# Prompt scores from three float32r products instead of one float32 product

## The chip, the cores and the metric

One Trainium2 chip, of which the kernel uses one core. The metric is the time of one execution on the device in microseconds (us); three timed executions of the kernel before took 1303.28, 1303.49 and 1303.51 us, median 1303.49 us.

## What is computed

The kernel does one inference step of a decoder trunk of two layers, for a prompt group (1 sequence of 256 tokens) and a sample group (8 sequences of 1 token) that share the weights. Each layer is a half feed-forward block, a mixer (a short convolution in layer 0, a gated linear recurrence in layer 1), a cross-attention on a memory, and a second half feed-forward block. The change lies in the cross-attention, which for the prompt is, per layer:

```python
def mem_kv(mem, g_mem, w_kv):
    k, v = jnp.split(rmsnorm(mem, g_mem) @ w_kv, 2, axis=-1)
    return k.reshape(B, N, X_HEADS, X_HEAD_DIM), v.reshape(B, N, X_HEADS, X_HEAD_DIM)

def cross_attn(x, mk, mv, w_q, w_o):
    q = (x @ w_q).reshape(B, T, X_HEADS, X_HEAD_DIM)
    s = jnp.einsum('bthd,bnhd->bhtn', q, mk.astype(q.dtype)).astype(jnp.float32) / math.sqrt(X_HEAD_DIM)
    p = jax.nn.softmax(s, axis=-1).astype(x.dtype)
    o = jnp.einsum('bhtn,bnhd->bthd', p, mv.astype(x.dtype)).reshape(B, T, D)
    return o @ w_o
```

Here D is 1024, T is 256, N (memory rows) is 256, and there are 4 heads of 256. The prompt's keys and values come from `mem_kv`, the samples' from a cache in HBM. Everything is float32.

## The kernel before, in words

The activations are kept transposed: `xT` has the 1024 model columns on 8 tiles of 128 partitions, and 264 columns, 256 of the prompt and 8 of the samples, so that every projection serves both groups. Nearly all products on TensorE use the type float32r, which is cheap there but keeps fewer bits. To keep the precision, an operand is split into a float32r part `h` and the float32r remainder `l` (`x - h`), and a product is made of three passes, h·h, h·l and l·h. `mm3` (L305 to L310) issues the three passes; in the projections they are L308, L309 and L310. The weights of a projection come from HBM as `raw`; ScalarE casts them to `wh` (L107), and VectorE or GpSimd subtracts to get `wl` (L119). The class `Weights` keeps this ahead of the products, five weight tiles deep.

In attention, `project` first makes the queries of the four heads, `qTs[h]` (L833, a VectorE multiplication out of PSUM, 256 head columns on two 128-partition tiles by 264 tokens, float32). Then, head by head, `do_kv` makes keys and values (L847 to L849, 512 columns a pass, 48 passes a head) and ScalarE copies them out to `Kn` and `Vn` (L857). During these four heads the weights' remainders `wl` are made by GpSimd (`W.lo = ("p",)`), otherwise by VectorE. At the end of `do_kv` the values are split into `Vh` (L864, ScalarE) and `Vl` (L865, VectorE).

The rest of a head runs beside the products of the next head. `Flow` holds three lanes of Python generators. After every few matmuls the program calls `flow.tick()`, which first advances the weights and then lets every lane take one step, up to its next `yield`. Lane 1 holds for each head: `transpose_k` (TensorE turns `Kn` into the PSUM tile `pkt`, L877, and VectorE copies it to `KTt`, L881); `prompt_scores` (the scores `psc`, L929, then the softmax: row maximum L913 and L914 on VectorE, exponentials L288 on ScalarE, L919 and L921 on VectorE into `Pp`; then TensorE turns `Pp` into `ppt`, L943, which is split into `PTh`, L949, and `PTl`, L950); and `prompt_values` (the output `po`, twelve passes of `mm3`, then its parts `oh`, L965, and `ol`, L966). From the transposing step of a head to its scores there are two more ticks in between. Lane 0 holds the samples' attention: for each head, 16 products of cached keys with the query on VectorE (`junk`, L901), and when all four heads are done `sample_rest`: the maximum over rows `mxs` (L973), turned by TensorE (`pst`, L976), the maximum `top` (L977), spread out to `tops` (L978), a product with `tops` (L980), and so on to the samples' values `spv` (L1003). The cached keys and values come through a ring of four buffers.

The steps of the program give each instruction its rank, but each engine's final order is made when the program is built, by rank and by what is estimated to be ready, and it is then fixed: on the chip, an engine takes its instructions strictly in that order. A tile with a tag and `bufs=1` has one place in memory; the next tile with that tag waits until all readers of the one before are done. In the score step `psc` is written by four float32 matmuls (two token halves, two head halves), each with a 128x128 part of `qT` as its weights and 256 columns of `KTt` moving.

Last comes the output projection (`out_proj`), in which VectorE makes `wl` again. The fourth head's turn, scores and values fall into it.

Of the kernel before, what the change touches and what calls it, by code (L numbers as in the profile page):

```python
# [8 lines left out]
F32 = mybir.dt.float32  # L9
F32R = mybir.dt.float32r  # L10
# [6 lines left out]
P = 128  # L17
D = 1024
KT = D // P
T = 256  # L20
# [4 lines left out]
NMEM = 256  # L25
# [196 lines left out]
def trunk_step(ctx: ExitStack, tc: tile.TileContext, ins, consts, outs, stop=None):  # L222
    nc = tc.nc
# [10 lines left out]
    def aux_bank(name):  # L234
        return paux.tile([P, 512], F32, tag="aux", name=name)
# [70 lines left out]
    def mm3(ps, w, rh, rl, first, last, s=slice(None)):  # L306
        wh, wl = w
        nc.tensor.matmul(ps, wh[:, s], rh, start=first, stop=False)  # L308
        nc.tensor.matmul(ps, wh[:, s], rl, start=False, stop=False)  # L309
        nc.tensor.matmul(ps, wl[:, s], rh, start=False, stop=last)  # L310
# [496 lines left out]
    def attention(l, norm, nxt):  # L807
        with tc.tile_pool(name="at", bufs=1) as ap:
            mh = ap.tile([P, KT, NMEM], F32R, name="mh")
            ml = ap.tile([P, KT, NMEM], F32R, name="ml")  # L810
            KTt, Vn, qTs, PTp = {}, {}, {}, {}
            oh = ap.tile([P, KT, NC], F32R, name="oh")
            ol = ap.tile([P, KT, NC], F32R, name="ol")
            sc = ap.tile([P, XH, NI], F32, name="sc")
# [24 lines left out]
            def do_kv(h):  # L839
# [25 lines left out]
                nc.vector.tensor_sub(vl, vn, vh.bitcast(F32))  # L865
                Vn[h] = vh, vl
                flow.spawn(1, transpose_k(h, kn))
                flow.spawn(1, prompt_scores(h))
                flow.spawn(1, prompt_values(h))
                flow.tick()  # L870

            def transpose_k(h, kn):
                yield
                pt = aux_bank("pkt")
                for dt in range(2):
                    for nt in range(2):
                        nc.tensor.transpose(  # L877
                            pt[:, dt * NMEM + nt * P : dt * NMEM + nt * P + P], kn[:, nt, dt * P : dt * P + P], ident
                        )
                KTt[h] = ap.tile([P, 2, NMEM], F32, tag="KTt", name=f"KTt{h}", bufs=1)  # L880
                nc.vector.tensor_copy(KTt[h], pt.rearrange("p (t n) -> p t n", t=2))  # L881
                yield
                yield

# [24 lines left out]
            def softmax(src, npart, rows, name):  # L909
                pr = ap.tile([npart, rows, NMEM], F32, tag=f"P{name}", name=f"P{name}", bufs=1)  # L910
                mx = ap.tile([npart, rows], F32, tag=f"mx{name}", name=f"mx{name}", bufs=2)
                zs = ap.tile([npart, rows], F32, tag=f"zs{name}", name=f"zs{name}", bufs=2)
                nc.vector.reduce_max(mx, src, axis=AX.X)  # L913
                nc.vector.tensor_scalar(mx, mx, -1.0 / 16.0, None, op0=ALU.mult)  # L914
                for r in range(rows):
                    act(
                        pr[:, r], src[:, r], AF.Exp, bias=mx[:, r : r + 1], scale=1.0 / 16.0, accum_out=zs[:, r : r + 1]
                    )
                nc.vector.reciprocal(zs, zs)  # L919
                for r in range(rows):  # L920
                    nc.vector.tensor_scalar(pr[:, r], pr[:, r], zs[:, r : r + 1], None, op0=ALU.mult)  # L921
                return pr

            def prompt_scores(h):
                qT = qTs[h]
                ps = aux_bank("psc")
                for tt in range(2):
                    for dt in range(2):
                        nc.tensor.matmul(  # L929
                            ps[:, tt * NMEM : tt * NMEM + NMEM],  # L930
                            qT[:, dt, tt * P : tt * P + P],
                            KTt[h][:, dt],
                            start=dt == 0,
                            stop=dt == 1,
                        )
                pr = softmax(ps.rearrange("p (t n) -> p t n", t=2), P, 2, "p")
                yield
                yield
                yield
                pt = aux_bank("ppt")  # L940
                for nt in range(2):
                    for tt in range(2):
                        nc.tensor.transpose(  # L943
                            pt[:, nt * T + tt * P : nt * T + tt * P + P], pr[:, tt, nt * P : nt * P + P], ident
                        )
                ptv = pt.rearrange("p (t n) -> p t n", t=2)
                th = ap.tile([P, 2, T], F32R, tag="PTh", name="PTh", bufs=1)
                tl = ap.tile([P, 2, T], F32R, tag="PTl", name="PTl", bufs=1)
                nc.scalar.copy(th, ptv)  # L949
                nc.vector.tensor_sub(tl, ptv, th.bitcast(F32))  # L950
                PTp[h] = th, tl
                yield
# [484 lines left out]
    for l in range(2):  # L1437
        plan.append(("norm_ffn1", l, SILU, ffn, lambda l=l: reg_ffn("ffn1", l)))
        plan.append(("norm_mix", l, None if l == 0 else SIGMOID, rec if l else conv, reg_rec if l else reg_conv))
        plan.append(("norm_xattn", l, None, lambda n, x, l=l: attention(l, n, x), lambda l=l: reg_att(l)))  # L1440
        plan.append(("norm_ffn2", l, SILU, ffn, lambda l=l: reg_ffn("ffn2", l)))
# [71 lines left out]
```

## Time and profile before

| what | value |
|---|---|
| median of three executions | 1303.49 us |
| the profiled execution, by its own time | 1303.28 us |
| span of the profiled execution, first to last instruction | 1301.3 us |
| TensorE matmul (PE) busy | 1279.6 us, 98% |
| VectorE (DVE) busy | 824.1 us, 63% |
| ScalarE (ACT) busy | 694.5 us, 53% |
| GpSimd (POOL) busy | 293.5 us, 23% |
| cross-attention, layer 0, queries to the fourth head's output | about 314 to 411 us |
| cross-attention, layer 1 | about 981 to 1078 us |
| granted TensorE clock, mean | 0.997 of full speed |

PE, DVE, ACT and POOL stand for TensorE, VectorE, ScalarE and GpSimd; L929 is line 929 of the kernel; `psc<-KTt,qT` names the tile written and the tiles read. Times count from the first instruction. The profile counts one float32 matmul as two instructions. [...]

### The profile page before, as it was taken

Reading aid. Unit: us, or ns where it says so; the run is one execution under the profiler, and the core shown is the slowest. Engines: PE = TensorE matmul, PEld = TensorE weight load, DVE = VectorE, ACT = ScalarE, POOL = GpSimd, SP = SyncE. Lnnn points to the kernel's source line nnn. Section 1 sums busy time; section 2 is a strip of 40 time slices with the busy share of each in tenths; the row PEclk is TensorE's granted clock in tenths of the full one; section 3 lists DMA queues with packets and bytes.
Section 4 is the critical chain, followed back from the end, with each engine's and each line's share of the span. In section 5 each row is a group of like instructions: output and inputs, shape, how many; then the busy total and the mean of one; then the engine's idle time right before and its main releaser. Section 6 shows DMA issues by size and latency. Waiting matters only on the chain.

```text
span 1301.3 us, 25953 instructions
## 1 busy us (share of the span) xinstructions
PE 1279.6 (98%) x10310; PEld 1236.4 (95%) x10310; DVE 824.1 (63%) x1570; ACT 694.5 (53%) x1146; POOL 293.5 (23%) x236
## 2 busy tenths in 40 slices
PE   8999999999999999999999999999999999999997
PEld 8999999999869999999999999999998779999996
DVE  6555567759826655556655545878789637766454
ACT  6454545446545645544554544656665447666542
POOL 3211231211741211132111132000023521211220
PEclk9999999999999999999999999999999999999998
DMA  8796555646997666556666556564557995776650
GB/s 269 245 302 178 166 182 175 208 142 201 357 379 218 195 180 178 185 164 201 179 178 186 176 175 186 157 195 136 169 157 257 394 327 160 223 215 198 204 167 34
DMA packets 263099, 266.75 MB, mean 205 GB/s; under 512 B 8697, under 2 KB 259577, under 8 KB 260930
## 3 DMA queue, kind: packets, MB, share of 16 engines
q1 hardware_dynamic: 257150, 259.78, 63.9%
q10 hardware_dynamic: 5828, 5.32, 1.2%
q8 instruction: 81, 1.33, 0.4%
q14 instruction: 40, 0.33, 0.1%
HBM read 255.00 MB, written 10.07 MB: 204 GB/s over the span
## 4 chain that ended last, share of the span: by engine, by line
PE 94%; DVE 3%; ACT 2%; issue 0%; DMA 0%; POOL 0%; DVEq 0%; SPq 0%; ACTq 0%; POOLq 0%
PE pj L308 20%; PE pj L309 19%; PE pj L310 19%; PE dn L308 7%; PE dn L310 7%; PE dn L309 7%; PE kv L847 2%; PE kv L849 2%; PE kv L848 2%; PE spv L1003 1%; PE psc L929 1%; PE pl L1163 1%; DVE wl L119 1%; PE pj L381 1%; DVE xl L332 1%; ACT wh L107 1%
## 5 line engine op out<-in xcount | busy, mean ns | idle before, releaser
L119 DVE TENSOR_TENSOR wl<-raw,wh 128x1024 fp32r<-128x1024 f32 (+1 forms) x347 | 426.6, 1234 | 248.8 <-ACT wh L107 238.0
L308 PE MATMUL pj<-xh,wh 128*128 128x264 f32 x1952 | 558.7, 286 | 2.3 <-DVE qT L833 2.3
L309 PE MATMUL pj<-xl,wh 128*128 128x264 f32 x1952 | 553.6, 284 | 0.0
L310 PE MATMUL pj<-xh,wl 128*128 128x264 f32 x1952 | 553.1, 283 | 0.0
L107 ACT CAST wh<-raw 128x1024 fp32r<-128x1024 f32 (+1 forms) x406 | 415.2, 1032 | 240.6 <-PE pj L309 108.3
L308 PEld LDWEIGHTS pj<-xh,wh 128*128 128x128 f32 x1952 | 367.8, 188 | 4.6 <-DVE qT L833 2.7
L309 PEld LDWEIGHTS pj<-xl,wh 128*128 128x128 f32 x1952 | 368.0, 189 | 0.0
L310 PEld LDWEIGHTS pj<-xh,wl 128*128 128x128 f32 x1952 | 366.2, 188 | 0.0
L308 PE MATMUL dn<-ah,wh 128*128 128x264 f32 x704 | 200.9, 285 | 0.0
L310 PE MATMUL dn<-ah,wl 128*128 128x264 f32 x704 | 200.0, 284 | 0.0
L309 PE MATMUL dn<-al,wh 128*128 128x264 f32 x704 | 199.4, 283 | 0.0
L119 POOL TENSOR_TENSOR wl<-raw,wh 128x1024 fp32r<-128x1024 f32 (+1 forms) x61 | 142.9, 2350 | 194.7 <-ACT wh L107 148.0
L703 POOL TENSOR_TENSOR al<-a,ah 128x264 fp32r<-128x264 f32 x88 | 90.1, 1026 | 415.6 <-ACT ah L702 415.5
L310 PEld LDWEIGHTS dn<-ah,wl 128*128 128x128 f32 x704 | 132.7, 188 | 0.0
L308 PEld LDWEIGHTS dn<-ah,wh 128*128 128x128 f32 x704 | 132.4, 188 | 0.2
L309 PEld LDWEIGHTS dn<-al,wh 128*128 128x128 f32 x704 | 132.5, 188 | 0.0
L288 ACT ACTIVATE g<-g 128x264 f32<-128x264 f32 x88 | 36.9, 424 | 78.9 <-DVE g L695 78.8
L702 ACT CAST ah<-a 128x264 fp32r<-128x264 f32 x88 | 36.0, 413 | 65.1 <-DVE a L701 64.3
L330 ACT ACTIVATE xh<-xT,gains 128x264 fp32r<-128x264 f32 x56 | 28.7, 513 | 75.9 <-DVE xT L729 59.2
L901 DVE CUSTOM_DVE_ANT_0 junk<-ring,pq 128x256 f32<-128x256 f32 x128 | 53.7, 420 | 3.7
L701 DVE TENSOR_TENSOR a<-g,pj 128x264 f32<-128x264 f32 x88 | 37.1, 426 | 29.0 <-PE pj L310 28.9
L695 DVE TENSOR_TENSOR g<-pj,R_norm_ffn 128x264 f32<-128x264 f32 x88 | 37.5, 429 | 28.1 <-PE pj L310 28.0
(329 smaller groups left out, 1494.3 us busy)
## 6 DMA issues: line engine op xcount, KB each, us to landing
raw<-in_w_ffn_gate_dram SPq DMA_DIRECT2D x88, 512.0 KB, 5.2
raw<-in_w_ffn_up_dram SPq DMA_DIRECT2D x88, 512.0 KB, 4.1
raw<-in_w_ffn_down_dram SPq DMA_DIRECT2D x64, 512.0 KB, 4.2
ring<-in_cache_mem_k_dram SPq DMA_DIRECT2D x16, 1024.0 KB, 6.6
raw<-in_w_xkv_dram SPq DMA_DIRECT2D x64, 256.0 KB, 3.6
ring<-in_cache_mem_v_dram SPq DMA_DIRECT2D x16, 1024.0 KB
raw<-in_w_rec_in_dram SPq DMA_DIRECT2D x32, 512.0 KB, 4.4
raw<-in_w_ffn_down_dram SPq DMA_DIRECT2D x32, 384.0 KB, 3.0
```

Of the source, the lines that this page charges most:

```text
L107: self.pin(copy(wh[:, :n], self.raw[i][:, :n]))
L119: ins = eng.tensor_sub(wl[:, :n], self.raw.pop(i)[:, :n], wh[:, :n].bitcast(F32))
L288: in_line(nc.scalar.activation(dst, src, func, **kw))
L308: nc.tensor.matmul(ps, wh[:, s], rh, start=first, stop=False)
L309: nc.tensor.matmul(ps, wh[:, s], rl, start=False, stop=False)
L310: nc.tensor.matmul(ps, wl[:, s], rh, start=False, stop=last)
L330: pin(nc.scalar.activation(h, src, AF.Copy, scale=g))
L695: nc.vector.tensor_mul(g, ps, norm.R)
L701: nc.vector.tensor_mul(a, g, ps)
L702: nc.scalar.copy(ah[:, blk], a)
L703: nc.gpsimd.tensor_sub(al[:, blk], a, ah[:, blk].bitcast(F32))
L901: nc.vector.tensor_tensor_reduce(junk, t[:, i % 8], pq[:, :XD], 1.0, 0.0, ALU.mult, ALU.add, sc[:, h, i : i + 1])
```

## The change

The float32 product of the scores is replaced by `mm3`: three float32r passes for each of the four products, twelve passes a head. For that the queries of a head are split into `qh` and `ql` at the start of `transpose_k` (256 of the 264 columns), and the turned keys are split into `kh` and `kl` instead of being copied to `KTt`. `qh` lies in the place of `PTh` (tag "PTh"), and `ql` in the place of `Pp` (tag "Pp"); both tags have one buffer. `kh` and `kl` have places of their own.

```diff
             def transpose_k(h, kn):
+                qh = ap.tile([P, 2, T], F32R, tag="PTh", name="qh", bufs=1)
+                ql = ap.tile([P, 2, T], F32R, tag="Pp", name="ql", bufs=1)
+                nc.scalar.copy(qh, qTs[h][:, :, :T])
+                nc.vector.tensor_sub(ql, qTs[h][:, :, :T], qh.bitcast(F32))
+                qs[h] = qh, ql
                 yield
                 pt = aux_bank("pkt")
...
-                KTt[h] = ap.tile([P, 2, NMEM], F32, tag="KTt", name=f"KTt{h}", bufs=1)
-                nc.vector.tensor_copy(KTt[h], pt.rearrange("p (t n) -> p t n", t=2))
+                ptv = pt.rearrange("p (t n) -> p t n", t=2)
+                kh, kl = (ap.tile([P, 2, NMEM], F32R, tag=n, name=f"{n}{h}", bufs=1) for n in ("KTh", "KTl"))
+                nc.scalar.copy(kh, ptv)
+                nc.vector.tensor_sub(kl, ptv, kh.bitcast(F32))
+                KTt[h] = kh, kl
                 yield
                 yield
...
             def prompt_scores(h):
-                qT = qTs[h]
+                kh, kl = KTt[h]
                 ps = aux_bank("psc")
                 for tt in range(2):
                     for dt in range(2):
-                        nc.tensor.matmul(
-                            ps[:, tt * NMEM : tt * NMEM + NMEM],
-                            qT[:, dt, tt * P : tt * P + P],
-                            KTt[h][:, dt],
-                            start=dt == 0,
-                            stop=dt == 1,
-                        )
+                        w = [q[:, dt] for q in qs[h]]
+                        s = slice(tt * P, tt * P + P)
+                        mm3(ps[:, tt * NMEM : tt * NMEM + NMEM], w, kh[:, dt], kl[:, dt], dt == 0, dt == 1, s)
```

(One more line adds the dictionary `qs`.)

More of the change, by code (lines that the diff above doesn't have):

```diff
@@ L810, in attention @@
             ml = ap.tile([P, KT, NMEM], F32R, name="ml")
-            KTt, Vn, qTs, PTp = {}, {}, {}, {}
+            KTt, Vn, qTs, qs, PTp = {}, {}, {}, {}, {}
             oh = ap.tile([P, KT, NC], F32R, name="oh")
```

## The prediction, made before the changed kernel was run

> **What bounds the kernel now.** I read the page first, for the engine that bounds, then the tile view of `psc`, then the timelines around the eight places where a head's keys are turned and scored.
>
> ```profile
> PE 1279.6 (98%) x10310; PEld 1236.4 (95%) x10310; DVE 824.1 (63%) x1570; ACT 694.5 (53%) x1146; POOL 293.5 (23%) x236
> ...
> PE 94%; DVE 3%; ACT 2%; issue 0%; DMA 0%; POOL 0%; DVEq 0%; SPq 0%; ACTq 0%; POOLq 0%
> ```
>
> TensorE makes up 94% of the chain that ended last. So a pass saved on TensorE is time saved, and a stop of TensorE is time lost, one for one, unless a later stop gets shorter by it; the other engines count only where TensorE waits for them.
>
> **TensorE's passes.** The scores before:
>
> ```profile
> L929 PE MATMUL psc<-KTt,qT x64: 377/379/463, 343.2 to 1068.1; 128*128 128x256 f32 x64
> ```
>
> 64 instructions are 8 heads of 8. Their own 379 ns overlap, so the price is read from starts. The first head of layer 0, and the twelve three-part passes of `po`, which have the shape that the new scores will have (128x128 weights, 256 columns moving, float32r):
>
> ```profile
> 343.22 1.89 PE L929 MATMUL psc<-KTt,qT 128*128 128x256 f32 x8
> 344.76 0.58 PE L847 MATMUL kv<-wh,mh 128*128 128x512 f32 x1
> 345.18 0.39 PE L848 MATMUL kv<-wl,mh 128*128 128x512 f32 x1
> ...
> 352.30 0.28 PE L308 MATMUL po<-PTh,Vh 128*128 128x256 f32 x1
> ...
> 353.73 0.39 PE L847 MATMUL kv<-wh,mh 128*128 128x512 f32 x1
> 353.97 0.40 PE L848 MATMUL kv<-wl,mh 128*128 128x512 f32 x1
> ```
>
> From the first `psc` to the second `kv` after it are 345.18 - 343.22 = 1.96 us. A `kv` pass in an undisturbed row takes 0.24 (353.97 - 353.73), so the eight instructions cost 1.72 to 1.73 us, the slow first `kv` included. The twelve passes of `po` cost 353.73 - 352.30 = 1.43 us, 0.119 each, with no slow follower. So the change takes 0.30 us a head off TensorE, 2.4 us over 8 heads. That is the whole gain: 0.18% of the time, just under the 0.2% (2.6 us) that a measurement of this kernel can tell from no change.
>
> [...]
>
> **What the other engines get.** Per head:
>
> ```profile
> L865 DVE TENSOR_TENSOR Vl<-Vn,Vh 128x512 fp32r<-128x512 f32 x3 | 2.1, 690 | 5.4 <-ACT Vh L864 5.4
> L881 DVE COPY KTt<-pkt 128x512 f32<-128x512 f32 x3 | 2.1, 685 | 1.5 <-PE pkt L877 1.5
> L864 ACT CAST Vh<-Vn 128x512 fp32r<-128x512 f32 x3 | 1.9, 619 | 2.5 <-PE po L310 1.9 <-ACT Vn L857 0.7
> L949 ACT CAST PTh<-ppt 128x512 fp32r<-128x512 f32 x3 | 1.8, 586 | 0.5 <-PE ppt L943 0.5
> ```
>
> `qh` is a cast like `Vh` (0.62 us on ScalarE), `kh` one like `PTh` (0.59, ScalarE), `kl` costs VectorE what the removed copy did (0.69), and `ql` is new work like `Vl` (0.69, VectorE). Neither engine is full, so their busy time costs nothing by itself. What costs is order: `psc` now waits for `qh`, `ql`, `kh` and `kl`, where it waited for one copy. The shared places make `qh` wait until the head before has done its last `po` pass, since those read `PTh`; `oh` waits for the same passes just ahead of it on ScalarE. `ql` in the place of `Pp` waits for `ppt` of the head before, long done. `Pp` and `PTh` of the same head come after its scores anyway and wait for nothing new. No DMA is added, removed or moved.
>
> **The second head, the place that decides.** The second head of layer 0, engine by engine (VectorE, ScalarE, GpSimd, TensorE):
>
> ```profile
> 357.01 0.67 DVE L966 TENSOR_TENSOR ol<-po,oh 128x512 fp32r<-128x512 f32 x1
> 357.61 0.64 DVE L978 COPY tops<-top 4x128 f32<-4x128 f32 x1
> 358.18 0.67 DVE L881 COPY KTt<-pkt 128x512 f32<-128x512 f32 x1
> ...
> 354.53 1.05 ACT L107 CAST wh<-raw 128x1024 fp32r<-128x1024 f32 x1
> 355.49 0.57 ACT L965 CAST oh<-po 128x512 fp32r<-128x512 f32 x1
> 356.74 1.06 ACT L107 CAST wh<-raw 128x1024 fp32r<-128x1024 f32 x1 [0.68 <-issue]
> ...
> 355.66 4.84 POOL L119 TENSOR_TENSOR wl<-raw,wh 128x1024 fp32r<-128x1024 f32 x2 [2.06 <-ACT wh L107]
> ...
> 358.31 0.38 PE L980 MATMUL pst<-ident,tops 4*128 4x4 f32 x2 [0.17 <-DVE tops L978]
> ...
> 359.43 1.46 PE L929 MATMUL psc<-KTt,qT 128*128 128x256 f32 x6
> ```
>
> `KTt` is ready at 358.85, only 0.58 us before `psc`, and TensorE already waits 0.17 us for `tops` at L980. `tops` has 4x128 elements and takes 0.64 us, ending just as the first of GpSimd's two subtractions ends (355.66 + 2.42 = 358.08). Other rows show why:
>
> ```profile
> 161.47 2.35 DVE L729 TENSOR_TENSOR xT<-xT,t 128x264 f32<-128x264 f32 x1
> ...
> 161.13 2.40 POOL L119 TENSOR_TENSOR wl<-raw,wh 128x1024 fp32r<-128x1024 f32 x1 [4.52 <-ACT wh L107]
> ...
> L332 DVE SCALAR_TENSOR_TENSOR xl<-xT,gains,xh x56: 483/495/1002, 159.1 to 1094.5; 128x264 fp32r<-128x264 f32 x56
> ...
> 293.01 2.81 DVE L332 SCALAR_TENSOR_TENSOR xl<-xT,gains,xh 128x264 fp32r<-128x264 f32 x3
> ...
> 292.23 3.31 POOL L341 TENSOR_TENSOR nacc_norm_xattn<-nacc_norm_xattn,nsq 128x264 f32<-128x264 f32 x3 [15.93 <-ACT nsq L340]
> ```
>
> A VectorE operation with both inputs in SBUF that starts while GpSimd works ends only shortly after GpSimd's does: 161.47 + 2.35 = 163.82 against 161.13 + 2.40 = 163.53. And when both have a queue, they take turns: three `xl` against three GpSimd additions took 2.81 us, 0.94 each in place of 0.495. An operation with an input in PSUM isn't held: `ol` took 0.67 in the middle of GpSimd's work.
>
> `ql` has both inputs in SBUF (`qT` and `qh`). `Vl` has too, and its row shows 0.69 and no hold; but `Vl` needs `Vh`, which ScalarE makes just ahead of the `wh` that GpSimd waits for, so it is through before GpSimd starts. `ql` comes behind that: `qh` follows `oh`, from 356.06 to 356.67, and GpSimd has been running since 355.66. [...]
>
> So `ql` is held until 358.1, or meets GpSimd's second subtraction (until 355.66 + 4.84 = 360.50), by its place on VectorE:
> - `ql` ahead of `tops`: it runs from 358.1 to 358.7; GpSimd's second subtraction takes its turn to 361.1; `tops` ends behind it, and L980 starts at 361.2 to 361.3 where it started at 358.31: TensorE stands 2.9 to 3.0 us.
> - `ql` behind `tops`: held until 360.50, done at 361.1; `kl`, behind it, is done one pitch (357.61 - 357.01 = 0.60) later plus its tail, at 361.8; `psc` starts at 361.85 where it started at 359.43: 2.4 us.
>
> In both, what is queued on VectorE behind `ql` is what TensorE needs next. Against it: each engine's order is made anew, and `psc` may be put behind some `kv` passes if its parts are expected later; the 0.60 us that `ql` adds is worth about three passes of 0.24. That takes up to 0.7 off the smaller case. I take 2.5 us, with bounds of 1.7 and 3.0. Layer 1 has the same pattern:
>
> ```profile
> 1024.42 0.66 DVE L978 COPY tops<-top 4x128 f32<-4x128 f32 x1
> ```
>
> its `tops` is as slow as layer 0's, so it counts twice: 5.0 us (3.4 to 6.0).
>
> **The other heads.** Third and fourth (GpSimd, ScalarE, TensorE; then VectorE, ScalarE, TensorE):
>
> ```profile
> 377.17 2.38 POOL L119 TENSOR_TENSOR wl<-raw,wh 128x1024 fp32r<-128x1024 f32 x1 [5.73 <-DMA ring<-in_cache_mem_v_dram]
> ...
> 377.00 0.58 ACT L965 CAST oh<-po 128x512 fp32r<-128x512 f32 x1
> ...
> 381.59 1.89 PE L929 MATMUL psc<-KTt,qT 128*128 128x256 f32 x8
> ...
> 397.63 1.22 DVE L119 TENSOR_TENSOR wl<-raw,wh 128x1024 fp32r<-128x1024 f32 x1
> ...
> 396.68 0.57 ACT L965 CAST oh<-po 128x512 fp32r<-128x512 f32 x1
> ...
> 399.74 1.89 PE L929 MATMUL psc<-KTt,qT 128*128 128x256 f32 x8
> ```
>
> Third head: `ql` is held until 379.55, done at 380.2, `kl` at 380.8, before 381.59: free, by 0.7 us of cover. Fourth head: GpSimd is idle there. `qh` ends at 397.85 and `kh` at 398.4; `wl`, which can now start at 396.8, ends at 398.0; then `ol`, `ql` and `kl` at a pitch of 0.60 end at about 399.85, against 399.74: 0.1 us (0 to 0.3), twice 0.2.
>
> First head:
>
> ```profile
> 340.18 0.62 ACT L864 CAST Vh<-Vn 128x512 fp32r<-128x512 f32 x1 [0.67 <-ACT Vn L857]
> 340.71 2.21 ACT L107 CAST wh<-raw 128x1024 fp32r<-128x1024 f32 x2
> ...
> 317.08 0.41 ACT L892 COPY zq<-qT 128x256 f32<-128x256 f32 x1 [0.36 <-PE pq L896]
> ```
>
> `qh` needs only the query here, and such work may be put early, as `zq` of the second head was (317.08, before the first head's products were through). If `kh` stands ahead of the second `wh`, it ends by 342.3 and `kl` by 343.0, before `psc` at 343.22: nothing. Behind it, third rival.
>
> **Sum**, against the profiled execution's own 1303.28 us: - 2.4 + 5.0 + 0.2 = + 2.8, 1306.1. The median of the runs lies 0.2 higher, so 1306.3 (bounds by the second and fourth heads: + 1.0 to + 4.2, 1304.5 to 1307.7). In the first and third head I cost the cast `kh` and the subtraction `ql` at nothing, since `kv` passes run on TensorE until `psc` is due; without that cover a head would pay 0.6 + 0.7 us.
>
> **Rivals.**
> - *The cover holds* (not slower): `ql` gets through ahead of GpSimd, or the order on TensorE puts enough `kv` passes ahead of L980 and `psc`. For it: `Vl` was never held; TensorE's waits in this stage are short now. Against it: GpSimd's start at 355.66 comes from the `wh` ahead of `oh` on ScalarE, and `qh` is behind both. Then the 2.4 us stay: 1301.1. It decides where `ql` costs less than 1.2 us a layer.
> - *More places*: in the first head `kh` stands behind the second `wh` (ends 342.92, later by `qh`'s 0.5), so `kh` ends at 343.5 to 344.0, `kl` at 344.2 to 344.7, and `psc` is 1.0 to 1.5 us late. Twice 1.2 on top of the forecast: 1308.7.
> - *The passes aren't cheaper*: `psc` keeps 0.216 us a pass, 12 x 0.216 = 2.59 in place of 1.73, + 6.9 in place of - 2.4: 1315.6. `po`'s rows speak against it.
>
> **Numbers.** The forecast, slower by holding VectorE in the second head, 0.57; the cover 0.28; more places 0.12; no cheaper passes 0.03. Half of the forecast's own range lies above + 2.6 us (0.31), half within (0.26). The cover gives 0.16 within and 0.12 faster, if something else gains a little; the others are slower. So faster 0.12, same 0.42, slower 0.46. The range from 1301.0 to 1308.6 leaves out the better part of the cover's gains and the upper half of the two dear rivals.
>
> **What would show it.** `psc` as 12 instructions of about 0.12 us each; `ql` of the second head taking well over 0.69 us while GpSimd runs, in both layers; a wait of TensorE of 2 us or more at L980 or at `psc` behind VectorE; no wait in the third head. I'm wrong if `ql` shows 0.69 us there, or if it is held and TensorE still waits for nothing; then the kernel should be 2 us faster.

## The result, and the profile after

The changed kernel took 1318.42 us, median of five executions (1314.66 to 1318.69), beside 1303.49 us before: a ratio of 1.0105 (95% interval 1.0094 to 1.0116). That is slower by 14.9 us; 2.8 us were forecast, and 1308.6 was the top of the range. The profiled execution is the quickest of the five, 1314.66 us, 11.4 us over the profiled one of before. First the page's busy line and the shares of its chain:

```profile
PE 1284.2 (98%) x10342; PEld 1239.1 (94%) x10342; DVE 838.2 (64%) x1578; ACT 703.4 (54%) x1162; POOL 294.7 (22%) x236
...
PE 92%; DVE 5%; ACT 2%; issue 1%; DMA 0%; POOL 0%; DVEq 0%; SPq 0%; ACTq 0%; POOLq 0%
```

The chain has moved 2 points from TensorE to VectorE. If the products outside attention (`pj`, `dn`) are laid side by side with those of before, their starts are equal up to layer 0's attention, 5.6 us late after it, still 5.6 us late up to layer 1's, and 11.4 us late from there to the end. So the whole loss lies in the two attentions, in equal parts. What TensorE waits for (us in total, times, the longest):

```profile
PE pst L984 <- DVE tops L982: 3.7, 2, 1.9
...
PE spv L1007 <- PE psc L310: 1.8, 2, 1.0
...
PE ppt L947 <- DVE Pp L929: 1.4, 2, 0.7
```

L984 is the product with `tops` (L980 before), and stands 1.84 and 1.90 us where it stood 0.17. The other two rows are new. The second names `psc` as what ended the wait, but `spv` reads `Ps`, and the timeline of the second head shows that (VectorE, GpSimd, TensorE):

```profile
357.82 0.21 DVE L977 TENSOR_REDUCE mxs<-sc 128x4 f32<-128x64 f32 x1
357.94 1.36 DVE L876 TENSOR_TENSOR ql<-qT,qh 128x512 fp32r<-128x512 f32 x1
359.23 0.27 DVE L981 TENSOR_REDUCE top<-pst 4x8 f32<-4x128 f32 x1
359.54 2.06 DVE L982 COPY tops<-top 4x128 f32<-4x128 f32 x1
...
365.45 2.45 DVE L994 SCALAR_TENSOR_TENSOR Ps<-sc,rzs,own 128x128 f32<-128x128 f32 x4
...
356.27 5.25 POOL L119 TENSOR_TENSOR wl<-raw,wh 128x1024 fp32r<-128x1024 f32 x2 [3.72 <-DMA raw<-in_w_xkv_dram]
364.60 2.36 POOL L119 TENSOR_TENSOR wl<-raw,wh 128x1024 fp32r<-128x1024 f32 x1 [3.08 <-ACT wh L107]
...
361.65 0.38 PE L984 MATMUL pst<-ident,tops 4*128 4x4 f32 x2 [1.84 <-DVE tops L982]
...
367.21 0.81 PE L1007 MATMUL spv<-ring,Ps 128*8 128x256 f32 x4 [0.86 <-PE psc L310]
```

`ql` is held, and GpSimd's second subtraction takes its turn behind it, as foretold. `tops` then ends at 361.60, just behind GpSimd's end at 356.27 + 5.25 = 361.52. But `tops` isn't late because of `ql` in the main: `mxs`, which starts ahead of `ql`, stands at 357.82 where the kernel before has 355.83, and `top` at 359.23 where it has 356.81. So of the 2.42 us by which `top` is late, 1.99 were there before `ql` began. The first of four `Ps` is held in the same way by the next subtraction, which ends at 366.96, and `spv` starts at 367.21. The first head has such a place too, the scaling of the prompt's probabilities:

```profile
348.70 1.52 DVE L929 TENSOR_SCALAR Pp<-Pp,zsp 128x256 f32<-128x256 f32 x2
...
347.41 2.40 POOL L119 TENSOR_TENSOR wl<-raw,wh 128x1024 fp32r<-128x1024 f32 x1 [0.85 <-ACT wh L107]
...
350.11 0.30 PE L947 MATMUL ppt<-ident,Pp 128*128 128x128 f32 x1 [0.72 <-DVE Pp L929]
```

The row holds two instructions; the first starts while GpSimd works and ends just behind it (349.81), after 1.27 us where the tile view's median is 0.35. Last, the windows around the stop at `tops` (the last three columns are the granted TensorE clock, the DMA share and GB/s):

```profile
360.00:362.00 2.00, 0.35 (x3) 0.34 (x3) 1.59 (x1) 0.00 (x0) 1.52 (x1) 1.00 1.11 413
362.00:365.00 3.00, 3.00 (x14) 2.68 (x13) 0.76 (x2) 2.26 (x9) 0.40 (x1) 0.58 1.01 402
365.00:368.00 3.00, 2.14 (x12) 1.40 (x12) 2.73 (x6) 0.00 (x0) 1.96 (x1) 0.85 1.05 370
```

Right after the stop the clock is granted at half: in the trace's clock records for 3.41 us, from 362.5 to 365.9, and so once in layer 1. The profile of before has no such window in attention. By the granted 0.5, 3.41 us do the work of 1.7, an estimate.

So layer 0's + 5.6 us are: stops + 3.3 (0.72 at `ppt`, 1.84 - 0.17 at `tops`, 0.86 at `spv`), the clock + 1.7, the cheaper passes - 1.2, and a rest of + 1.8. Most of this rest is no stop at all. The samples' values `spv` are 128 instructions a layer; before, their first sixteen stand in one piece, and in the changed kernel other products come in between:

```profile
362.63 1.05 PE L1003 MATMUL spv<-ring,Ps 128*8 128x256 f32 x16
```

```profile
367.21 0.81 PE L1007 MATMUL spv<-ring,Ps 128*8 128x256 f32 x4 [0.86 <-PE psc L310]
...
368.38 0.60 PE L1007 MATMUL spv<-ring,Ps 128*8 128x256 f32 x2
...
369.33 1.03 PE L1007 MATMUL spv<-ring,Ps 128*8 128x256 f32 x10
```

In one piece they start in groups of four, 7 ns apart, a group every 0.2 us; broken up, a single one takes 0.2 us too. TensorE is busy with `spv` for 8.40 us a layer before and for 9.79 after, 1.4 us more. The last 0.4 us are not assigned.

### The profile page after: what moved, and what is told of

Its sections match the earlier page's. It is cut to its first block, busy times and chain, and to the rows that moved or that the text cites. A ratio compares the mean times of both kernels' runs of the same rounds, so it can differ in the third digit from the quotient of the medians.

```text
span 1312.7 us, 26045 instructions
## 1 busy us (share of the span) xinstructions
PE 1284.2 (98%) x10342; PEld 1239.1 (94%) x10342; DVE 838.2 (64%) x1578; ACT 703.4 (54%) x1162; POOL 294.7 (22%) x236
## 4 chain that ended last, share of the span: by engine, by line
PE 92%; DVE 5%; ACT 2%; issue 1%; DMA 0%; POOL 0%; DVEq 0%; SPq 0%; ACTq 0%; POOLq 0%
PE pj L308 19%; PE pj L309 19%; PE pj L310 19%; PE dn L308 7%; PE dn L310 7%; PE dn L309 6%; PE kv L847 2%; PE kv L849 2%; PE kv L848 2%; PE spv L1007 1%; PE pl L1167 1%; DVE wl L119 1%; PE pj L381 1%; DVE xl L332 1%; DVE junk L909 1%
```

## The experiments

After the result the theory read: the stop at `tops` is the forecast's own mechanism, and `ql`, made late because its place is shared, starts it all. The rivals: the shared place has nothing to do with it; any additional work on VectorE does it; the clock, not the stop, is the larger part. "Before" is always the kernel before, on the same chip.

**The queries' high part in a place of its own.** To make room, two other tiles (`gs`, `sconv1`) share one.

```diff
-                qh = ap.tile([P, 2, T], F32R, tag="PTh", name="qh", bufs=1)
+                qh = ap.tile([P, 2, T], F32R, tag="qh", name="qh", bufs=1)
```

> The changed kernel with one place of its own for qh (tag qh, one buffer) in place of PTh's; ql stays in Pp. Theory (the subtraction ql comes to VectorE late, because qh has to wait in PTh's place for the po passes of the head before, and is then held by GpSimd with tops queued behind it): ql of the second head runs well before tops, TensorE waits under 0.5 us at the product with tops in both layers, the clock stays at 1.00 through the stage, and the time falls from 1318 to 1301 to 1303 us, at or below the kernel before. Rival (the pair kh, kl is the cost: psc waits for a cast and a subtraction where it waited for one copy): the wait moves to psc and the time stays above 1310. Rival (the halved clock comes from the mix of passes, not from a stop): the clock still drops twice and the time stays above 1306.

It took 1313.87 us beside 1303.52, ratio 1.0081 (1.0066 to 1.0096). TensorE's waits:

```profile
PE spv L1007 <- DVE Ps L994: 3.3, 2, 1.6
...
PE po L309 <- DVE PTl L954: 2.5, 4, 0.9
PE pst L984 <- DVE tops L982: 2.5, 2, 1.2
```

The second head's `ql` now runs at 351.91, before `tops`, but is held there too (2.08 us) and makes `PTl` late, and `tops` is held 1.50 us all the same. The shared place isn't the cause; its removal only moves the holds.

**The parts made, and not read.** The kernel before, with `qh` and `ql` made in the shared places, and the scores still in float32 from `KTt` and `qT`.

```diff
+                qh = ap.tile([P, 2, T], F32R, tag="PTh", name="qh", bufs=1)
+                ql = ap.tile([P, 2, T], F32R, tag="Pp", name="ql", bufs=1)
+                nc.scalar.copy(qh, qTs[h][:, :, :T])
+                nc.vector.tensor_sub(ql, qTs[h][:, :, :T], qh.bitcast(F32))
```

> The kernel before, with its float32 scores, and qh and ql made in the shared places as in the change, but read by nobody. Theory: the hold of ql and the turn that tops loses behind it need no new scores, so the product with tops stops TensorE for about 1.8 us a layer, the clock drops to half after it, and the time is 10 to 16 us above the kernel before (1313 to 1319). Rival (kh, kl): nothing waits for qh and ql, 1303 to 1305. Rival (order of the passes of psc): the same, 1303 to 1305.

1311.38 us (1311.06 to 1312.3), ratio 1.0061 (1.0046 to 1.0076): `ql` held 1.82 us, `tops` 1.56, with stops of 0.47 us at `psc`, 0.79 at the product with `tops` and 0.57 at `spv`. Slower by 7.9 us without a single new pass, so a loss of this kind doesn't need the new scores.

**No `ql`.** The third pass and `ql` are left out, so that the scores are made of two products, eight passes a head.

```diff
-                ql = ap.tile([P, 2, T], F32R, tag="Pp", name="ql", bufs=1)
...
-                nc.vector.tensor_sub(ql, qTs[h][:, :, :T], qh.bitcast(F32))
```

> The changed kernel without ql: the third pass (keys' h part by the queries' l part) is left out, so the scores are made of eight passes a head; qh stays in PTh's place, kh and kl stay. Theory: without ql nothing is held ahead of tops; TensorE waits under 0.5 us there, the clock stays up, and each head costs 8 x 0.119 = 0.95 us in place of 1.73, so 1303.5 - 6.2 = 1297 us (1296 to 1300). Rival (kh, kl): a stop of 1 us or more at psc of the second head remains and the time is above 1303. Rival (the shared place of qh alone): above 1303 too.

1310.49 us (1310.33 to 1312.78), ratio 1.0059 (1.0042 to 1.0075), with 3.8 us less of passes than the changed kernel. The theory fell here: `tops` is held without `ql`. The second head's rows (VectorE, GpSimd):

```profile
357.22 0.21 DVE L976 TENSOR_REDUCE mxs<-sc 128x4 f32<-128x64 f32 x1
358.33 0.28 DVE L980 TENSOR_REDUCE top<-pst 4x8 f32<-4x128 f32 x1 [0.90 <-PE pst L979]
358.64 2.03 DVE L981 COPY tops<-top 4x128 f32<-4x128 f32 x1
...
355.87 4.72 POOL L119 TENSOR_TENSOR wl<-raw,wh 128x1024 fp32r<-128x1024 f32 x2 [3.78 <-ACT wh L107]
```

and the same of the kernel before, with its first head's `Pp` and GpSimd's work beside it:

```profile
348.32 0.62 DVE L921 TENSOR_SCALAR Pp<-Pp,zsp 128x256 f32<-128x256 f32 x2
355.83 0.21 DVE L973 TENSOR_REDUCE mxs<-sc 128x4 f32<-128x64 f32 x1
356.81 0.28 DVE L977 TENSOR_REDUCE top<-pst 4x8 f32<-4x128 f32 x1 [0.76 <-PE pst L976]
...
348.82 4.78 POOL L119 TENSOR_TENSOR wl<-raw,wh 128x1024 fp32r<-128x1024 f32 x2 [2.16 <-ACT wh L107]
```

Before, `Pp` was through at 348.94, just after GpSimd had started (348.82), and `tops` started at 357.61, in GpSimd's first subtraction, which ended at 358.08. Here `Pp` is held (TensorE's wait at `ppt` is 0.7 as in the changed kernel), VectorE has two of the samples' products left where it had none, `ol` comes ahead of `mxs`, and `top` is 1.52 us later. So `tops` starts at 358.64, in the second subtraction, and waits for its end at 360.59. With `ql` or without it, 1 us decides whether `tops` meets the end of one subtraction or the start of another.

**Work while TensorE waits.** Sixteen unread passes a layer (1.9 us) in `sample_rest`.

```diff
+                pb = mm_bank("busy")
+                for i in range(16):
+                    nc.tensor.matmul(pb[:, :T], mh[:, i % KT, :P], mh[:, i % KT], start=True, stop=True)
```

> The changed kernel with 16 more passes of 128x256 (1.9 us of TensorE) a layer in sample_rest, after the turning of mxs, into a bank that nobody reads. They stand some passes ahead of the stop at tops, so they move TensorE's queue back while tops is being held. Theory of the clock (TensorE's stop, not the work, is what halves the clock afterwards): the stop shrinks by most of 1.8 us, the clock stays at 1.00 or drops once, and the time falls to 1307 to 1313 in spite of 3.8 us more work. Rival (the stop is only a stop): the time stays at 1318 or rises by up to 3.8 us.

1306.48 us (1306.32 to 1307.83), ratio 1.0023 (1.0014 to 1.0033): 11.9 us quicker than the changed kernel, with 3.8 us more of passes. But the order changed: `tops` now takes 0.21 us, and there is no stop to fill. What it does show is that in attention stop and halved clock left together (clock 1.00 from 314 to 414 us and from 1034 to 1040), and that the cheaper passes are worth what they were forecast: here `spv` takes 8.40 us as before, only the first head's stop of 0.72 us is left, and 3.8 - 2.4 + 2 x 0.72 = 2.8 us, where 3.0 were measured. The question of the clock stayed open.

**Three small steps out of PSUM.** The exponentials go to PSUM (to `psc` itself, and to `pst` for the samples), and `top` does too. So `Pp`'s scaling, `tops` and `Ps` have an input in PSUM.

```diff
-                    nc.vector.tensor_scalar(pr[:, r], pr[:, r], zs[:, r : r + 1], None, op0=ALU.mult)
+                    nc.vector.tensor_scalar(pr[:, r], src[:, r], zs[:, r : r + 1], None, op0=ALU.mult)
...
-                top = ap.tile([XH, NB], F32, name="top")
...
+                top = pt[:XH, 2 * P : 2 * P + NB]
```

> The changed kernel, with its shared places, but three small VectorE steps take their input from PSUM in place of SBUF: the exponentials of the prompt's scores stay in psc and are scaled from there into Pp, top lies in pst and is spread from there into tops, the samples' exponentials lie in pst and are spread from there into Ps. Same engines, same number of instructions. Theory two (what stops TensorE is that these three steps, which only touch SBUF, are held by GpSimd's subtractions wl; ql is only one more that is held): tops takes under 0.3 us, Pp 0.35 to 0.5 each, Ps under 0.4 each; TensorE's stops at ppt, tops and spv vanish, one at pst or psc behind the held ql may stay (up to 1.4 us a layer), the clock stays up, and the time is 1301 to 1306. Rival (VectorE simply has too much to do, so the samples' chain ends late): the three steps get shorter and the time stays above 1309.

1305.39 us (1302.95 to 1308.06, ten executions) beside 1303.87, ratio 1.0008 (0.9998 to 1.0017). The tile view of `tops` (ns: least, median, most):

```profile
L982 DVE COPY tops<-pst x2: 277/278/278, 359.5 to 1026.4; 4x128 f32<-4x128 f32 x2
```

Of the 14.9 us 13.0 are back, and TensorE stops nowhere in the first three heads, while `ql` is still held up to 1.9 us. So a held `ql` alone costs TensorE nothing here; the holds of the three small steps are the cause of the stops.

**The same edit in the kernel before.**

> The kernel before with the same three steps reading PSUM: the control. Theory two: in the kernel before only 0.35 us of TensorE stops hang on them in both layers, so 1302.5 to 1304 us. If the steps from PSUM are a gain of their own, it shows here.

1311.32 us (1308.73 to 1313.9), ratio 1.0053 (1.0037 to 1.0069): a miss. In it TensorE waits 0.65 us for the fourth head's `Pp` in each layer, the mean granted clock is 0.995 (0.997 in the profile of before), and `spv` takes 9.6 us a layer for 8.4. Why its order came out worse wasn't found.

**The kernel before, with `KTt` copied twice.** No split, no `ql`, 0.6 us more on VectorE per head.

```diff
                 nc.vector.tensor_copy(KTt[h], pt.rearrange("p (t n) -> p t n", t=2))
+                nc.vector.tensor_copy(KTt[h], pt.rearrange("p (t n) -> p t n", t=2))
```

> The kernel before with the copy KTt made twice in every head: 0.6 us more of VectorE a head, no other work, no split, float32 scores. Theory two (the kernel before stands at a lucky alignment of GpSimd's subtractions and the small steps; any delay of VectorE or any other order loses it): 4 us or more slower, 1308 to 1315, with tops or Pp held for over 1 us. Rival (ql and its hold are the cost): under 1 us slower, 1303 to 1304.5.

1310.77 us (1310.19 to 1315.15), ratio 1.0056 (1.0038 to 1.0074). Its second head (VectorE, GpSimd, TensorE):

```profile
360.50 0.69 DVE L881 COPY KTt<-pkt 128x512 f32<-128x512 f32 x1 [0.16 <-PE pkt L877]
361.11 2.03 DVE L979 COPY tops<-top 4x128 f32<-4x128 f32 x1
...
358.23 4.83 POOL L119 TENSOR_TENSOR wl<-raw,wh 128x1024 fp32r<-128x1024 f32 x2 [3.58 <-ACT wh L107]
...
363.20 0.38 PE L981 MATMUL pst<-ident,tops 4*128 4x4 f32 x2 [1.56 <-DVE tops L979]
```

`KTt`, 128 times as many bytes but read from PSUM, takes its 0.69 us in the midst of GpSimd's work; `tops` behind it ends with GpSimd (363.06). So the kernel before stands on an alignment that a little added work can upset, and 7 us hang on it.

**Both remedies at once, own place and PSUM.**

> f2_three_psum with the place of its own for qh, so that ql stands early on VectorE, ahead of the remainder PTl of the first head. Theory two: the four stops of the run with the own place alone (ppt, PTl, tops, Ps) fall to the one at PTl behind ql (0.9 us a layer), and the clock stays up: 1301 to 1305 us. Rival (VectorE too full): above 1309.

1307.96 us (1306.96 to 1313.03), ratio 1.0036 (1.0024 to 1.0047). `PTl`, queued behind the early held `ql`, stops TensorE 1.3 us in each layer, and the fourth head's `Pp` 0.65: the own place is worse than the shared one.

**GpSimd's subtractions cut.** If a hold lasts as long as GpSimd's instruction, shorter instructions must shorten it. In the stage of the keys and values, GpSimd makes each `wl` in two pieces of 1.3 us, or in four of 0.76.

```diff
-        ins = eng.tensor_sub(wl[:, :n], self.raw.pop(i)[:, :n], wh[:, :n].bitcast(F32))
+        raw = self.raw.pop(i)
+        m = self.cut if n % self.cut == 0 and eng is nc.gpsimd else 1
+        for a in range(0, n, n // m):
+            c = slice(a, a + n // m)
+            ins = eng.tensor_sub(wl[:, c], raw[:, c], wh[:, c].bitcast(F32))
```

> The changed kernel, with each of GpSimd's subtractions wl in the key and value stage issued as two of half the size (1.2 us each in place of 2.4). VectorE's work is untouched. Theory two (GpSimd's long subtractions hold VectorE's steps between SBUF and SBUF): no step is held longer than about 1.3 us, tops falls from 2.06 to 1.4 us or less, the stop of TensorE behind it from 1.84 to 1.0 us or less, and the time lies between 1304 and 1313. Rival (VectorE too full): the holds shrink, the time stays at 1314 to 1319.

> The same in four subtractions of 0.6 us. Theory two: holds of 0.7 us at most, stop behind tops under 0.5 us, no halved clock from it, 1301 to 1307. Rival: 1314 to 1319. If the four pieces cost GpSimd much more than 2.4 us together, the weights come late and a new wait for wl shows.

> Control: the kernel before with GpSimd's subtractions in two. Theory two with the lucky alignment: its 0.17 us stop at tops may vanish, or the new order may lose the alignment, 1302.5 to 1308; it is not expected to gain more than 0.5 us.

The tile view of `tops`, cut in two, then in four:

```profile
L987 DVE COPY tops<-top x2: 977/978/978, 359.7 to 1030.1; 4x128 f32<-4x128 f32 x2
```

```profile
L987 DVE COPY tops<-top x2: 439/442/444, 358.7 to 1027.0; 4x128 f32<-4x128 f32 x2
```

With subtractions of 2.4, 1.3 and 0.76 us `tops` takes 2.06, 0.98 and 0.44 us, and the kernel 1318.42, 1310.9 (ratio 1.0052, 1.0037 to 1.0067) and 1305.95 us (1.0018, 1.0009 to 1.0028). The kernel before cut in two doesn't change: 1304.12, ratio 1.0002 (0.9992 to 1.0011). So it isn't GpSimd's total work, which even rises with the cuts (294.7, 300.4 and 310.1 us), but the length of one instruction.

**PSUM and cuts together, in two and in four.**

> The three steps reading PSUM (as in f2) and GpSimd's subtractions in two. What is left to be held is ql, now for 1.2 us at most. Theory two: 1301 to 1305, with less spread from run to run than f2 if the stops of the fourth head don't grow.

> The three steps reading PSUM and GpSimd's subtractions in four: all that the earlier runs showed to shorten the holds, together. Theory two: ql held for 0.6 us at most, no stop of TensorE over 0.2 us in the first three heads, and the saving of the cheaper passes is left: 1301 to 1304, below the kernel before if the clock stays up in the fourth head.

1305.6 us (1302.76 to 1307.97), ratio 1.0010 (1.0000 to 1.0020), and 1305.89 us (1302.94 to 1308.41), ratio 1.0012 (1.0002 to 1.0022). None of all these versions beats the kernel before by its median. Two things use up the saved 2.4 us. The first needs no stop: `spv` takes 9.21 us a layer with PSUM alone or with the cut in two, 9.46 with the cut in four and 10.17 with the cuts alone, for 8.40 before; so layer 0 of the kernel with PSUM and four pieces, from its first `kv` to the first product behind the fourth head's `po`, takes 82.96 us at full clock, and 82.88 before. The second stands in its profile in the fourth head of layer 1:

```profile
1073.00:1080.00 7.00, 5.31 (x24) 4.58 (x25) 1.38 (x2) 1.17 (x2) 0.00 (x0) 0.66 0.53 187
```

The fourth head has no other products to run beside it, and TensorE stops there some 0.7, 0.34 and 0.68 us in every kernel, that of before included. In this execution the clock falls to half for some 6.8 us (0.66 from 1073 to 1080 us, 0.83 from 1080 to 1086). The executions differ roughly as their mean clock does: 1302.94 and 1303.21 us at 0.998, 1304.62 at 0.996, 1305.89 at 0.995, 1306.81 at 0.993, 1308.41 at 0.992. Even the quickest lies only 0.3 us below the quickest of the kernel before beside it (1303.24).

**A stop of the same cause, filled.** To part the clock from the stop: 15 unread passes a layer (1.8 us), bound to a place right ahead of the product with `tops`.

```diff
+                spr = nc.vector.reduce_max(top, pt[:XH, :P].rearrange("h (b g) -> h b g", b=NB), axis=AX.X)
...
+                pb = mm_bank("busy")
+                for i in range(15):
+                    b4 = nc.tensor.matmul(pb[:, :T], mh[:, i % KT, :P], mh[:, i % KT], start=True, stop=True)
+                    order(b4, spr.ins, "inside the stop")
```

> The changed kernel with 15 more passes of 128x256 a layer (1.8 us, into a bank that nobody reads), put right ahead of the product with tops, that is into the stop itself. The hold of tops is untouched. Clock theory (the halved clock follows from TensorE standing still, and is worth some 4 of the 15 us): tops still takes about 2 us, the stop before it shrinks to 0.8 us or less, the clock isn't halved behind it, and in spite of 3.6 us more work the time falls to 1309 to 1314, with less spread. Rival (the time is lost by the stops alone): 1318 or more.

1310.84 us (1310.61 to 1311.93) beside 1304.26, ratio 1.0054 (1.0041 to 1.0066). `tops` is held as long as ever, and the clock stays whole in the same window:

```profile
L982 DVE COPY tops<-top x2: 2101/2101/2101, 359.7 to 1030.2; 4x128 f32<-4x128 f32 x2
```

```profile
362.00:365.00 3.00, 3.00 (x20) 2.73 (x21) 1.41 (x6) 1.27 (x8) 0.00 (x0) 1.00 1.06 421
```

The stop that is left is 0.57 us. In the profiled executions it is 3.9 us quicker than the changed kernel (1314.66 - 1310.79): the passes cost 3.6, the stops at `tops` get 2.6 shorter, the stops at `spv`, which are gone, give 1.8, and the clock's two windows of 1.7 give 3.4, together - 4.2. By the medians it is 7.6 us quicker, so in the usual execution of the changed kernel, at a clock of 0.992 to 0.993, the clock takes, by this estimate, some 7 us and not 3.4; those executions have no profile.

## Why the prediction was wrong

*The passes:* right. The third head's scores of the changed kernel, first and last pass and the follower:

```profile
387.55 0.28 PE L308 MATMUL psc<-KTh,qh 128*128 128x256 f32 x1
...
388.87 0.28 PE L310 MATMUL psc<-KTh,ql 128*128 128x256 f32 x1
388.99 0.40 PE L847 MATMUL kv<-wh,mh 128*128 128x512 f32 x1
```

Twelve passes in 1.44 us, as against 1.43. The rival of dear passes is out; the third head costs nothing, and the fourth head's stop grows by 0.06 us, about as foretold.

*"The second head, the place that decides":* right that VectorE's steps are held by GpSimd there, and nearly right in size: `ql` is held (1.36 us), GpSimd's second subtraction takes its turn, `tops` ends behind it, and TensorE stops there in both layers, 1.84 and 1.90 us for the 2.5 of the forecast. But the step fails in two ways. It holds `ql` responsible, and the run without `ql` and the one with a second copy show `tops` held 2.03 us without it; in the changed kernel itself 1.99 of the 2.42 us by which `top` is late were there before `ql` began. The sum was made with `ql`'s 0.69 us, where any shift of about 1 us would do, so that the near fit of the size is in part luck. And it calls one place the one that decides. The view was narrowed to operations "with both inputs in SBUF", though the row that it quoted, `tops` at 0.64, is a copy with one input, held by GpSimd. The scaling of `Pp` has one input tile too; with it the first head stops 0.72 us, and with `Ps` the samples' values 0.86 to 0.96. Both places were in no term. Reading these steps from PSUM took all the stops of the first three heads away (`tops` takes 2.06 us from SBUF and 0.28 from PSUM).

*The first head:* "nothing" was wrong, as was the rival's reason for the opposite (`kh` behind `wh`). What came instead is a changed order on ScalarE that starts GpSimd at 347.41 and not 348.82, just ahead of `Pp`.

*The sum:* it has no term for the clock. A stop was priced at its own length, "one for one". A stop of 1.84 us took 1.7 us more by a window at half clock in the profiled execution and, by the estimate above, about twice that in the others. This is the largest single omission, some 7 of the 12 us by which the forecast was short. Nor has it a term for a new grouping of TensorE's other products, and `spv` alone costs 1.4 us a layer more.

*The range:* apart from the passes that aren't cheaper, the dearest case (1308.7) was a sum of stops in named places, with the order otherwise kept. The copy made twice shows that an added 0.6 us a head, by itself, costs 6.9 us; no case was made for the order falling anew.

What isn't settled: why the order breaks `spv` up in most of these kernels (the filled stop has 9.66 us, the work while waiting 8.40), and why it comes out worse when the PSUM edit is made in the kernel before.

## What to carry to other kernels

Where GpSimd runs long instructions (2.4 us each here), list every VectorE step that touches only SBUF, however small (`tops`, 4x128 elements, took 2.06 us, and 0.28 from PSUM), and look where each would fall if the order moved by a microsecond; read such steps from PSUM, or cut GpSimd's instructions, before work is added. Look also at products that stand packed together before and broken up after: here they cost 0.8 to 1.8 us a layer with no stop to be seen. Price a stop of TensorE of about 2 us with a range up to twice its length or more, as the clock may be halved behind it (here for 3.41 us behind 1.84). And when a kernel has rows like `tops` (0.64 us for 4x128 elements, ending with GpSimd's instruction), its present time hangs on an alignment: copy one small step twice to see how much.

## What the runs showed of the hardware

A stop of 1.84 us was followed by 3.41 us of the clock granted at half. In two profiles (the three steps out of PSUM, alone and with the cut in four) the fourth head's stops of 0.68 and 0.34 us, close together, were followed by some 6.8 us at half, which began before the third stop; with PSUM and the cut in two the same stops had none (mean granted clock 0.998, and 0.995 in the other two). Not every longer stop is followed by one: the own place's stops of 1.24 and 1.64 us had none in their profile (clock 1.00 from 340 to 384 us), nor had the filled stop's 0.72 and 0.57 us (1.00 from 340 to 384 us); the unread parts' 0.47, 0.79 and 0.57 us, close together, had one in layer 0 (0.83 from 362 to 372 us), and none in layer 1 (1.00 from 1012 to 1044 us) with stops of nearly the same lengths.

So the length of a stop doesn't decide it alone. The run without `ql` stops 1.76 us at `tops` in both layers: in layer 0 the `kv` passes behind it start 0.41 to 0.43 us apart from 361.73 on, as in the changed kernel's window at half (0.43), and in layer 1 0.22 to 0.24 apart from 1032.50 on. In the clock records of the changed kernel's profile the moments at which the granted clock changes inside the kernel are whole multiples of 3.413 us apart (362.49 and 1034.91 by 197 times that). Whether it matters how a stop lies between such moments was not shown. The executions of the version with PSUM and four pieces spread over 5.5 us, at mean clocks of 0.998 to 0.992; only the profiled one shows where the clock fell.

Short float32 products with 8 columns of weights started in groups of four when they stood in one piece, 7 ns apart in a group and 0.2 us from group to group: sixteen `spv` instructions took 1.05 us, and 2.44 us in the pieces of four, two and ten of the changed kernel.
